# Ranking the background work of a one-core layer kernel 120 instructions behind its matmuls

## The chip, the core and the metric

The kernel runs on one core of a Trainium2 chip. The metric is the device time of one execution in microseconds (us); the time before is the median of three runs, 2014.33 us. The engines are named as in the profile: PE (TensorE, matmuls and transposes), DVE (VectorE), ACT (ScalarE), POOL (GpSimd) and SP, whose queue issues the DMAs.

## What is computed

One layer over 2048 tokens of width 1024, in float32:

```python
n = rms_norm(x, norm1_w)
q, k, v, g_lr, g_out, su, sv = split(n @ w_in)             # 256, 256, 512, 16, 512, 512, 512 columns
log_a = log_sigmoid(g_lr @ w_gate_up + b_gate_up) / 16
o = rms_norm(gla_chunked(q / 8, k, v, log_a), gla_norm_w) * silu(g_out)     # chunks of 64 tokens, state 64x128 per head
s = gelu(su) * (tril(w_s) @ layer_norm(gelu(sv)) + b_s)                     # chunks of 128 tokens
h = x + concat(o, s) @ w_out
h = h + (silu(n2 @ w_ffn_gate) * (n2 @ w_ffn_up)) @ w_ffn_down             # n2 = rms_norm(h, norm2_w)
out = rms_norm(h, final_norm_w)
```

## The kernel before

**Tiling.** The tokens are worked in four blocks of 512 rows: blocks 0 and 1, then the feed-forward part of both, then blocks 2 and 3 and theirs. A block is held transposed (`nT`, eight pieces of 128 features by 512 tokens). Each float32 operand is split into a rounded high part and a remainder: `split` (L100) casts on ACT (L104) and subtracts on DVE (L105). `mm3` (L125) makes one product from three matmuls (L128, L129, L130): low by high, high by low, high by high. Weights come by DMA into `rawp` (three buffers), their high and low parts stand in `wp` (eight buffers, four pairs). All matmul outputs share eight PSUM banks (`psp`), and a bank is free when the last engine that reads it is done.

**A block.** `mix` (L529) makes in turn the gate columns and the 16 columns of the low rank, the decay factors (`decay`, L561: two matmuls L567, then ACT and DVE in turn), k and q (`col_pair`), the products with the decay (L591, L592, L614), the values v and the output gate, a second half of the sv columns (`second_half`, L680, 128x256 outputs), then su. In blocks 1 to 3, v and the gate come from seven products instead of eight (`pair_product`, L222, in the order 1, 2, 7, 6, 4, 5, 3). The left sides of products 7, 5, 6 and 3 are sums of halves of `nT`, made step by step by `Halves.make` (L177 to L210: DVE additions L182, L196, L200, L204, L209, each followed by a split into `hop`). `drain` (L715) takes the outputs: for product 1 an ACT copy into v and for product 2 a DVE addition (L720); for product 5, once for each of two halves, an ACT copy (L731), an addition (L732) and a Silu (L733).

**The chunks.** `chunks` (L636) takes the 512 tokens in two halves. For each it makes 16 matmuls of keys by values (L645, into two banks `pu`) and 16 of scores (L654, into two banks `pq`). DVE then runs the state chain, 16 steps L663, each of which reads the step before and a piece of `pu`, and four masked copies L667 that read `pq`. `attend` (L746) multiplies states and scores (L762), normalises and transposes (L752).

**Rows to come.** `norm_rows` (L264) prepares the next block: for each 128 rows a squared sum on ACT, a scaling on DVE (L246) into one of two buffers `xsu`, eight transposes on PE (L253) and two splits of the PSUM outputs (ACT L104 and DVE L105, into `nTh` and `nTl`). The same generator serves the rows that go into the feed-forward part.

**What sets the order.** `norm_rows`, `Halves.make`, `decay`, `chunks`, `attend`, the sums of weights (L474) and others are generators in the list `bg`. `tick()` (L66) advances each of them by one step after each group of products; `finish` (L71) runs one to its end. When the program is built, a list scheduler fixes the order of every engine: of the instructions that its own estimate of times has ready, the one that stands first in program order goes first. On the chip each engine takes its instructions in that order, and each waits on semaphores for what it reads or overwrites. The start of the program (L341 to L401) is written out in the order of the work: a 4 KB row of norm weights is spread over the partitions by two matmuls (L364) and two copies (L366), with matmuls of zeros (`idling`, L357) around them.

Of the kernel before, what the change touches and what calls it, by code (L numbers as in the profile page):

```python
# [33 lines left out]
def hybrid_block(ctx, tc, x, norm1_w, w_in, w_gate_up, b_gate_up, gla_norm_w, sg_ln_w, sg_ln_b,  # L34
# [21 lines left out]
    def tpt(name, dt=F32):  # L56
        return tp.tile([P, 512], dt, name=name, tag="tp")
# [5 lines left out]

    bg = []

    def tick():  # L66
        for g in list(bg):
            if next(g, bg) is bg:
                bg.remove(g)

# [4 lines left out]

    def start(g):
        bg.append(g)
        return g

# [259 lines left out]
    n1 = sum(c for _, c in first_cols)  # L339
    blank = tpt("blank", BF16)  # L340
    nc.vector.memset(blank, 0.0)  # L341
    one_row = tpt("one")[0:1, :P]
    nc.vector.memset(one_row, 1.0)
    n1w = nwp.tile([P, D], F32, name="nw", tag="nw")
    nc.sync.dma_start(n1w[0:1, :], norm1_w[0].unsqueeze(0))
    hx = dma_x(x2, 0, [0])
    raws = []
    for t, (k0, kk) in enumerate(first_k):
# [5 lines left out]
        dma_x(x2, 0, [t + 1], hx)  # L354
    idle = ps()

    def idling(n):  # L357
        for _ in range(n):
            nc.tensor.matmul(idle, lhsT=blank[:, :P], rhs=blank, start=True, stop=True)

    idling(8)
    pw = [ps(), ps()]
    for i in range(2):
        nc.tensor.matmul(pw[i], lhsT=one_row, rhs=n1w[0:1, i * 512:(i + 1) * 512], start=True, stop=True)  # L364
    for i in range(2):
        nc.scalar.copy(n1w[:, i * 512:(i + 1) * 512], pw[i])  # L366
    idling(4)
    nT = Act(KD, "nT")
    xsu = bigt(F32, "xsu").rearrange("p (c a) b -> p c (a b)", c=2)
    first_w = []  # L370

# [10 lines left out]

    r0 = row_rstd(hx[0])
    for i in range(2):
        cs = slice(i * 512, (i + 1) * 512)
        nc.vector.scalar_tensor_tensor(xsu[:, 0, cs], hx[0][:, cs], r0, n1w[:, cs], ALU.mult, ALU.mult)
    first_split(raws[0])
    for i in range(2):
        first_put(0, i)
        idling(4)  # L390
    norm_prep(hx[1], n1w, xsu[:, 1])
    first_split(raws[1])
    first_split(raws[2])

# [7 lines left out]

    start(first_rows())

# [124 lines left out]
    def mix(blk, nT, first_w):  # L529
# [6 lines left out]
        def first_done(t, acc):  # L536
            g = glr[:, t]
            hi = sm.tile([P, RANK], F32R, name="glrhi")
            nc.scalar.copy(hi, acc[:, 256:256 + RANK])
            nc.vector.tensor_copy(g[:, 0:RANK], f32(hi))  # L540
            nc.vector.tensor_copy(g[:, 64:64 + RANK], f32(hi))
            nc.vector.tensor_tensor(g[:, 32:32 + RANK], acc[:, 256:256 + RANK], f32(hi), ALU.subtract)
            nc.scalar.activation(sv[:, t, 0:256], acc[:, 0:256], AF.Gelu)
            start(glr_put(t, g))

# [15 lines left out]
        def decay():  # L561
            yield
            if blk:
                yield
            pks = [ps(), ps()]
# [18 lines left out]

        g_dec = start(decay())

# [124 lines left out]
        else:  # L711
            gw = bigt(F32, "gw")
            started = []

            def drain(m, th, acc):  # L715
                lo, hi = th, 2 + th
                if m == 1:
                    nc.scalar.copy(v[:, lo, :], acc)
                elif m == 2:
                    nc.vector.tensor_tensor(v[:, lo, :], acc, v[:, lo, :], ALU.add)  # L720
                elif m == 7:
                    nc.scalar.copy(gw[:, hi, :], acc)
                elif m == 6:
                    nc.scalar.copy(v[:, hi, :], acc)
                elif m == 4:
                    nc.vector.tensor_tensor(v[:, hi, :], acc, v[:, hi, :], ALU.add)
                    if th:
                        started.append(chunks_start())
                elif m == 5:
                    x = tpt("x")  # L730
                    nc.scalar.copy(x, acc)  # L731
                    nc.vector.tensor_tensor(gw[:, hi, :], x, gw[:, hi, :], ALU.add)  # L732
                    nc.scalar.activation(gw[:, hi, :], gw[:, hi, :], AF.Silu)  # L733
                else:
                    gate_done(lo, acc)
# [48 lines left out]

        g_att = start(attend())

# [31 lines left out]
    def project(blk, hx, mixT, g_att, put, outer, ahead=None):  # L818
# [7 lines left out]
        def out_done(t, acc):  # L826
            residual(hx, 1, acc, t)
            r = blk * NB + t * P
            nc.sync.dma_start(hd[r:r + P, :], hx[t])
            if outer:  # L830
                gens.append(start(norm2_put(t, norm_prep(hx[t], n2w))))

# [80 lines left out]
    def gate_up(s, act):  # L913
# [59 lines left out]
        def run(late):  # L973
            for at, (key, _, m) in enumerate(seq):
                ahead(at + AHEAD + 1)
                if at == len(seq) - 5:
                    start(late)
                made[key].mul(m)
# [145 lines left out]
    for s in range(2):  # L1124
# [56 lines left out]

        start(first_operands())
        ahead, run = gate_up(s, tm)
# [13 lines left out]

        start(last_operands())
        d_start, d_run = down(s)
# [47 lines left out]
```

## Time and profile before

| | |
|---|---|
| median of three runs | 2014.33 us (2013.3 to 2014.34) |
| the profiled execution | 2013.45 us, of which the span is 2011.7 us and 1.75 us lie around it |
| PE busy | 1979.5 us, 98% of the span, mean granted clock 0.994 |
| DVE busy | 1493.7 us, 74% |
| ACT busy | 894.2 us, 44% |
| POOL busy | 86.2 us, 4% |
| DMA | 328.69 MB, mean 163 GB/s |

An engine is busy while an instruction runs on it. The start of one instruction to the start of the next on the same engine is what it costs there when nothing waits; the printed duration of a matmul is longer, since matmuls overlap. "idle before <-releaser" at a row is the time for which the engine waited in front of it, and the instruction that ended the wait. The clock is the granted share of TensorE's full 2.4 GHz; the lower of its two levels is 1.2 GHz.

### The profile page before, as it was taken

The page shows a single profiled execution, that of the slowest core. Times are in us where ns is not written, and L with a number is a line of the kernel's source. Part 1 is how long each engine was busy: PE and PEld are TensorE (multiplying, and loading weights), DVE is VectorE, ACT ScalarE, POOL GpSimd, SP SyncE. Part 2 cuts the span into 40 slices and gives each one's busy share as a digit, 9 for nine tenths or more (in the row PEclk, how much of TensorE's full clock was granted, in tenths as well). Part 3 has the DMA queues.
Part 4 walks back from the last instruction along what each step waited for, and adds up shares of the span by engine and source line. Part 5 has one row for each costly group of instructions (what it writes and reads, how often), then busy time and mean ns, then how long its engine had stood idle before and what let it go on. Part 6 is the DMA issues. An engine that isn't in the chain of part 4 may idle for free.

```text
span 2011.7 us, 26653 instructions
## 1 busy us (share of the span) xinstructions
PE 1979.5 (98%) x9861; PEld 1649.4 (82%) x9861; DVE 1493.7 (74%) x2516; ACT 894.2 (44%) x1475; POOL 86.2 (4%) x118
## 2 busy tenths in 40 slices
PE   8999899999999999999999998999999999999998
PEld 6888778888888888888887887887888888888887
DVE  6666887798987777655798758758977877776476
ACT  4544645453333333443565536446433333334343
POOL 2010101000000000000110101000000000000000
PEclk9999999999999999999999999999999999999999
DMA  6645385526663333865756444623332332367554
GB/s 211 179 159 167 137 266 175 189 89 195 219 204 97 120 98 127 302 199 179 246 181 202 137 129 155 210 84 112 114 115 94 105 115 95 100 209 266 189 190 176
DMA packets 216577, 328.69 MB, mean 163 GB/s; under 512 B 16712, under 2 KB 117630, under 8 KB 215424
## 3 DMA queue, kind: packets, MB, share of 16 engines
q1 hardware_dynamic: 216448, 327.00, 50.1%
q8 instruction: 77, 1.26, 0.3%
q14 instruction: 52, 0.43, 0.1%
HBM read 245.69 MB, written 77.07 MB: 160 GB/s over the span
## 4 chain that ended last, share of the span: by engine, by line
PE 85%; DVE 7%; ACT 4%; DMA 2%; issue 2%; POOL 0%; DVEq 0%; POOLq 0%; ACTq 0%; SPq 0%
PE ps L129 27%; PE ps L128 27%; PE ps L130 27%; DMA raw<-ad 1%; PE ps L762 1%; PE ps L253 1%; DVE b L1194 1%; DVE wlo L105 1%; DVE op L105 1%; DVE hx L1047 1%; ACT whi L104 1%; PE ps L800 1%; DMA raw<-in_w_ffn_down_dram 0%; DVE aop L105 0%; DVE sw L872 0%
## 5 line engine op out<-in xcount | busy, mean ns | idle before, releaser
L104 ACT CAST whi<-raw 128x1024 fp32r<-128x1024 f32 (+2 forms) x193 | 194.1, 1008 | 310.2 <-PE ps L129 138.2
L105 DVE TENSOR_TENSOR wlo<-raw,whi 128x1024 fp32r<-128x1024 f32 (+2 forms) x193 | 224.4, 1168 | 140.5 <-ACT whi L104 133.2
L129 PE MATMUL ps<-wlo,aop 128*128 128x512 f32 x552 | 215.1, 390 | 0.2 <-DVE wlo L105 0.2
L128 PE MATMUL ps<-whi,aop 128*128 128x512 f32 x552 | 215.1, 390 | 0.0
L130 PE MATMUL ps<-whi,aop 128*128 128x512 f32 x552 | 214.9, 389 | 0.0
L104 ACT CAST op<-sw 128x512 fp32r<-128x512 f32 x176 | 107.3, 621 | 210.6 <-DVE sw L872 190.4
L105 DVE TENSOR_TENSOR aop<-raw,aop 128x1024 fp32r<-128x1024 f32 x76 | 86.5, 1139 | 89.3 <-ACT aop L104 89.1
L105 DVE TENSOR_TENSOR op<-sw,op 128x512 fp32r<-128x512 f32 x176 | 120.2, 686 | 36.0 <-ACT op L104 35.8
L129 PE MATMUL ps<-wlo,nTh 128*128 128x512 f32 (+2 forms) x392 | 129.9, 331 | 12.0 <-DVE wlo L105 12.0
L128 PE MATMUL ps<-whi,nTl 128*128 128x512 f32 (+2 forms) x392 | 129.6, 332 | 3.2 <-DVE nTl L105 2.2
L130 PE MATMUL ps<-whi,nTh 128*128 128x512 f32 (+2 forms) x392 | 129.3, 330 | 0.0
L104 ACT CAST aop<-raw 128x1024 fp32r<-128x1024 f32 x76 | 74.5, 983 | 121.8 <-DMA raw<-ad 120.5
L129 PEld LDWEIGHTS ps<-wlo,aop 128*128 128x128 f32 x552 | 103.6, 188 | 22.0 <-DVE wlo L105 0.8
L128 PEld LDWEIGHTS ps<-whi,aop 128*128 128x128 f32 x552 | 103.7, 188 | 21.6
L130 PEld LDWEIGHTS ps<-whi,aop 128*128 128x128 f32 x552 | 103.7, 188 | 21.4
L105 DVE TENSOR_TENSOR op<-raw,op 128x512 fp32r<-128x512 f32 x132 | 88.5, 686 | 26.5 <-ACT op L104 25.9
L897 ACT COPY p<-ps 128x512 f32<-128x512 f32 x88 | 51.4, 587 | 127.4 <-PE ps L130 124.4
L128 PE MATMUL ps<-whi,mixTl 128*128 128x512 f32 x256 | 101.4, 396 | 0.9 <-DVE mixTl L105 0.9
L128 PE MATMUL ps<-nTh,wlo 128*128 128x512 f32 x256 | 101.8, 397 | 0.0
L925 ACT ACTIVATE cg<-cg 128x512 f32<-128x512 f32 x88 | 55.6, 632 | 100.1 <-DVE cg L924 100.0
L129 PE MATMUL ps<-nTl,whi 128*128 128x512 f32 x256 | 99.9, 390 | 0.0
L130 PE MATMUL ps<-nTh,whi 128*128 128x512 f32 x256 | 99.8, 390 | 0.0
(273 smaller groups left out, 5001.0 us busy)
## 6 DMA issues: line engine op xcount, KB each, us to landing
raw<-in_w_in_dram SPq DMA_DIRECT2D x66, 512.0 KB, 4.6
raw<-ad SPq DMA_DIRECT2D x64, 512.0 KB, 3.8
raw<-in_w_ffn_gate_dram SPq DMA_DIRECT2D x44, 512.0 KB, 3.9
raw<-in_w_ffn_up_dram SPq DMA_DIRECT2D x44, 512.0 KB, 3.8
raw<-td SPq DMA_DIRECT2D x35, 512.0 KB, 4.3
ad<-cg SPq DMA_DIRECT2D x66, 256.0 KB, 2.0
ad<-cs SPq DMA_DIRECT2D x22, 768.0 KB, 3.6
hx<-in_x_dram SPq DMA_DIRECT2D x32, 512.0 KB, 6.7
```

The costliest lines, as they stand in the source:

```text
L104: nc.scalar.copy(hi, src)
L105: nc.vector.tensor_tensor(lo, src, f32(hi), ALU.subtract)
L128: nc.tensor.matmul(o, lhsT=ll, rhs=rh, start=first, stop=False, skip_group_check=shared)
L129: nc.tensor.matmul(o, lhsT=lh, rhs=rl, start=False, stop=False, skip_group_check=shared)
L130: nc.tensor.matmul(o, lhsT=lh, rhs=rh, start=False, stop=last, skip_group_check=shared)
L253: nc.tensor.transpose(pt[:, k * P:(k + 1) * P], xs[:, (4 * i + k) * P:(4 * i + k + 1) * P], ident)
L762: nc.tensor.matmul(pos[hh][c * CH:(c + 1) * CH, (2 * i + p) * DV:(2 * i + p + 1) * DV], lhsT=left[:, hh, p, n * CH:(n + 1) * CH], rhs=righ ...
L800: nc.tensor.matmul(pm[:, t * P:(t + 1) * P], lhsT=sv[:, t, g * P:(g + 1) * P], rhs=wsT[:, g, :], start=True, stop=True)
L897: nc.scalar.copy(t[m], o)
L925: nc.scalar.activation(g, g, AF.Silu)
L1047: nc.vector.tensor_tensor(h[i, l], h[i, l], y, ALU.add)
L1194: nc.vector.tensor_tensor(*(b[:, k] for b in args[:3]), args[3])
```

## The change

Each step that `tick()` makes is put 120 places further back in the order by which the scheduler chooses, save for generators that are started as urgent. These are the first rows, the transposes of the low rank (`glr_put`), `decay`, `attend`, the second norm of blocks 1 and 3 (`norm2_put`) and the late operands of the feed-forward part. `decay` drops one step in blocks 1 to 3. In `drain` of product 5 both ACT copies come ahead of both additions. The start is written inside `tc.manual_schedule()`, which keeps the written order on each engine: the norm weights come as one DMA to all partitions (512 KB), the matmuls L364 and copies L366 go, and 24 matmuls of zeros stand where 20 stood.

```diff
+    LATER = 120
+    bg, urgent = [], []
     def tick():
         for g in list(bg):
-            if next(g, bg) is bg:
-                bg.remove(g)
+            with tc.high_priority(offset=0 if g in urgent else -LATER):
+                if next(g, bg) is bg:
+                    bg.remove(g)
...
-    def start(g):
+    def start(g, now=False):
         bg.append(g)
+        if now:
+            urgent.append(g)
...
-    n1w = nwp.tile([P, D], F32, name="nw", tag="nw")
-    nc.sync.dma_start(n1w[0:1, :], norm1_w[0].unsqueeze(0))
-    hx = dma_x(x2, 0, [0])
...
-    idling(8)
-    pw = [ps(), ps()]
-    for i in range(2):
-        nc.tensor.matmul(pw[i], lhsT=one_row, rhs=n1w[0:1, i * 512:(i + 1) * 512], start=True, stop=True)
-    for i in range(2):
-        nc.scalar.copy(n1w[:, i * 512:(i + 1) * 512], pw[i])
-    idling(4)
...
+    with tc.manual_schedule():
+        blank = tpt("blank", BF16)
+        nc.vector.memset(blank, 0.0)
+        hx = dma_x(x2, 0, [0])
+        n1w = norm_w(norm1_w[0])
+        first_load(*first_k[0])
+        first_load(*first_k[1])
+        dma_x(x2, 0, [1], hx)
+        first_load(*first_k[2])
+        dma_x(x2, 0, [2, 3], hx)
...
+        idling(18)
+        r0 = row_rstd(hx[0])
...
+        first_put(0, 0)
+        idling(3)
+        nc.vector.tensor_tensor(lo, raws[0], f32(hi), ALU.subtract)
+        first_w.append((hi, lo))
+        first_put(0, 1)
+        idling(3)
+        first_split(raws[1])
+        norm_prep(hx[1], n1w, xsu[:, 1])
+        first_split(raws[2])
...
-    start(first_rows())
+    start(first_rows(), True)
...
-            start(glr_put(t, g))
+            start(glr_put(t, g), True)
...
         def decay():
             yield
-            if blk:
-                yield
...
-        g_dec = start(decay())
+        g_dec = start(decay(), True)
...
                 elif m == 5:
-                    x = tpt("x")
-                    nc.scalar.copy(x, acc)
-                    nc.vector.tensor_tensor(gw[:, hi, :], x, gw[:, hi, :], ALU.add)
-                    nc.scalar.activation(gw[:, hi, :], gw[:, hi, :], AF.Silu)
+                    kept.append(tpt("x"))
+                    nc.scalar.copy(kept[th], acc)
+                    for i in range(2) if th else ():
+                        g = gw[:, 2 + i, :]
+                        nc.vector.tensor_tensor(g, kept[i], g, ALU.add)
+                        nc.scalar.activation(g, g, AF.Silu)
...
-        g_att = start(attend())
+        g_att = start(attend(), True)
```

Lines of the changed kernel are numbered five higher up to `decay`, three higher from there to the `drain` of product 5, and five higher behind it: L110 is the subtraction L105, L187, L205, L209 and L214 are the additions L182, L200, L204 and L209, L258 is the transpose L253, L648 and L657 are the chunk products L645 and L654, L666 is the step of the state chain L663, L723 is the addition L720.

At three places the orders stand as follows. The first is DVE in block 1, between the left operands of the chunks and the additions of product 2 to the values. `hs` and `nw` are scratch of `Halves`, `hop` a made left side, `wlo` the low part of a weight. Before:

```order
L204 TENSOR_TENSOR nw<-nw,hs 128x1024
L591 TENSOR_TENSOR eu<-ps,eu 128x512
L592 TENSOR_TENSOR eu_2097<-ps,eu_2097 128x512
L105 TENSOR_TENSOR hop<-nw,hop 128x1024
L614 SCALAR_TENSOR_TENSOR left<-ps,eu 64x512 x4
L105 TENSOR_TENSOR wlo<-raw,whi 128x1024
L209 TENSOR_TENSOR hs<-hs,nw 128x1024
L105 TENSOR_TENSOR wlo<-raw,whi 128x1024 x2
L105 TENSOR_TENSOR hop<-hs,hop 128x1024
L105 TENSOR_TENSOR wlo<-raw,whi 128x1024
L720 TENSOR_TENSOR v<-ps,v 128x512 x2
```

Now, the twelve rows that follow `left`, `wlo`, `hop` and two more `wlo`:

```order
L187 TENSOR_TENSOR nw<-nTh_1538,nTl_1540 128x1024
L110 TENSOR_TENSOR wlo<-raw,whi 128x1024
L205 TENSOR_TENSOR nw<-nw,hs 128x1024
L110 TENSOR_TENSOR wlo<-raw,whi 128x1024
L187 TENSOR_TENSOR hs<-nTh_1538,nTl_1540 128x1024
L110 TENSOR_TENSOR hop<-nw,hop 128x1024
L110 TENSOR_TENSOR wlo<-raw,whi 128x1024
L209 TENSOR_TENSOR nw<-nw,hs 128x1024
L214 TENSOR_TENSOR hs<-hs,nw 128x1024
L110 TENSOR_TENSOR wlo<-raw,whi 128x1024
L723 TENSOR_TENSOR v<-ps,v 128x512 x2
L110 TENSOR_TENSOR hop<-nw,hop 128x1024
```

The steps of `Halves` that stood ahead of the left operands stand behind them, and so do four more `wlo`; the two additions L723 and the `hop` of product 6 come last.

The second is PE in block 1 around the chunk products (x16 is 16 in a row). Before, for the first half; the second half stood 48 matmuls of products 5 and 3 (three to a row of `mm3`, all left operand `hop`) further back, and then the 128x256 outputs of `second_half`:

```order
L130 MATMUL ps<-whi,nTh_1539 128x512
L623 MATMUL ps<-ident,eu_2097 128x128 x2
L645 MATMUL ps<-v,eu_2097 64x128 x16
L654 MATMUL ps<-left,eu 64x64 x16
L128 MATMUL ps<-whi,hop 128x512
L129 MATMUL ps<-wlo,hop 128x512
```

Now:

```order
L134 MATMUL ps<-wlo,hop 128x512
L135 MATMUL ps<-whi,hop 128x512
L648 MATMUL ps<-v,eu_2096 64x128 x13
L657 MATMUL ps<-left,eu 64x64 x16
L648 MATMUL ps<-v,eu_2096 64x128 x16
L657 MATMUL ps<-left,eu 64x64 x16
L133 MATMUL ps<-whi,nTl_1539 128x256
L134 MATMUL ps<-wlo,nTh_1537 128x256
```

Both halves stand behind product 3, next to each other, ahead of `second_half`; three of the L648 of the first half stand ahead of product 6.

The third is PE at the transition from block 0 to block 1. Before, the last of four groups of eight transposes, the other three of which stood 24 matmuls apart in front of it:

```order
L128 MATMUL ps<-whi,mixTl_1245 128x512
L129 MATMUL ps<-wlo,mixTh_1243 128x512
L130 MATMUL ps<-whi,mixTh_1243 128x512
L253 MATMUL ps<-ident,xsu 128x128 x8
L128 MATMUL ps<-whi,nTl_1540 128x272
L129 MATMUL ps<-wlo,nTh_1538 128x272
```

Now:

```order
L133 MATMUL ps<-whi,mixTl_1244 128x512
L134 MATMUL ps<-wlo,mixTh_1242 128x512
L135 MATMUL ps<-whi,mixTh_1242 128x512
L258 MATMUL ps<-ident,xsu 128x128 x29
L133 MATMUL ps<-whi,nTl_1539 128x272
L134 MATMUL ps<-wlo,nTh_1537 128x272
```

The transposes of all four groups of rows but three stand in one piece between the output projection of block 0 and the first columns of block 1. The transition from block 2 to block 3 reads the same.

## Rows read from the trace of the kernel before

**Rows 1.** The page, busy time of each engine and its share of the span

```profile
PE 1979.5 (98%) x9861; PEld 1649.4 (82%) x9861; DVE 1493.7 (74%) x2516; ACT 894.2 (44%) x1475; POOL 86.2 (4%) x118
```

**Rows 2.** The page, chain that ended last, by engine

```profile
PE 85%; DVE 7%; ACT 4%; DMA 2%; issue 2%; POOL 0%; DVEq 0%; POOLq 0%; ACTq 0%; SPq 0%
```

**Rows 3.** Timeline of PE, blocks 1 to 3: start us, us, instruction, [idle before <-releaser]

```profile
227.56 0.71 PE L567 MATMUL ps<-glrT,wup 96*128 96x512 f32 x2
...
251.57 0.80 PE L129 MATMUL ps<-wlo,nTh 128*128 128x512 f32 x1 [4.77 <-DVE wlo L105]
252.16 0.63 PE L130 MATMUL ps<-whi,nTh 128*128 128x512 f32 x1
252.59 0.63 PE L128 MATMUL ps<-whi,nTl 128*128 128x512 f32 x1
...
288.59 0.50 PE L128 MATMUL ps<-whi,hop 128*128 128x512 f32 x1 [2.56 <-ACT x L731]
...
1067.57 0.76 PE L129 MATMUL ps<-wlo,nTh 128*128 128x512 f32 x1 [2.48 <-DVE wlo L105]
1243.68 0.80 PE L129 MATMUL ps<-wlo,nTh 128*128 128x512 f32 x1 [4.77 <-DVE wlo L105]
1403.52 0.47 PE L129 MATMUL ps<-t3l,op 128*128 128x512 f32 x1 [1.56 <-ACT op L104]
```

**Rows 4.** Stretches: length; busy us (xcount) of PE, PEld, DVE, ACT, POOL; PE clock; DMA

```profile
240.00:260.00 20.00, 14.86 (x59) 11.71 (x57) 17.86 (x23) 12.18 (x16) 0.00 (x0) 0.83 0.57 214
1060.00:1080.00 20.00, 17.01 (x68) 13.22 (x67) 17.24 (x27) 12.84 (x19) 1.73 (x1) 0.91 0.46 154
1400.00:1420.00 20.00, 18.44 (x82) 14.99 (x81) 20.00 (x34) 8.29 (x15) 0.00 (x0) 1.00 0.16 54
```

**Rows 5.** Timeline of PE, transition from block 0 to block 1

```profile
200.47 0.39 PE L130 MATMUL ps<-whi,mixTh 128*128 128x512 f32 x1
200.70 1.03 PE L253 MATMUL ps<-ident,xsu 128*128 128x128 f32 x8
201.49 0.37 PE L128 MATMUL ps<-whi,nTl 128*128 128x272 f32 x1
```

**Rows 6.** Timeline of DVE, same transition

```profile
203.31 1.28 DVE L105 TENSOR_TENSOR nTl<-ps,nTh 128x512 fp32r<-128x512 f32 x2
204.51 1.28 DVE L246 SCALAR_TENSOR_TENSOR xsu<-hx,st,nw 128x1024 f32<-128x1024 f32 x1
```

**Rows 7.** Timeline of DVE, block 1: left operands and the value additions

```profile
246.32 1.23 DVE L105 TENSOR_TENSOR hop<-nw,hop 128x1024 fp32r<-128x1024 f32 x1
247.47 2.79 DVE L614 SCALAR_TENSOR_TENSOR left<-ps,eu 64x512 f32<-64x512 f32 x4
...
257.66 0.69 DVE L720 TENSOR_TENSOR v<-ps,v 128x512 f32<-128x512 f32 x1
```

**Rows 8.** Timeline of DVE, block 1: state chain and masks of one half

```profile
279.96 2.99 DVE L663 SCALAR_TENSOR_TENSOR right<-right,dec,ps 64x128 f32<-64x128 f32 x8
282.87 0.92 DVE L667 COPY_PREDICATED left<-keep,ps 64x256 f32<-64x256 int32 x2
```

**Rows 9.** Timeline of PE, block 1: both sorts of chunk product, then the next columns

```profile
293.12 1.16 PE L645 MATMUL ps<-v,eu 64*64 64x128 f32 x32
294.05 1.15 PE L654 MATMUL ps<-left,eu 64*64 64x64 f32 x32
295.13 0.39 PE L128 MATMUL ps<-whi,nTl 128*128 128x256 f32 x1
```

**Rows 10.** Timeline of PE, block 0: one transpose between large products

```profile
45.80 0.48 PE L128 MATMUL ps<-nTh,wlo 128*128 128x512 f32 x1
46.12 0.40 PE L129 MATMUL ps<-nTl,whi 128*128 128x512 f32 x1
```

**Rows 11.** Timeline of PE, start of the program

```profile
4.80 3.78 PE L364 MATMUL ps<-nw,one 1*128 1x512 f32 x4
...
13.27 1.04 PE L380 MATMUL ps<-ident,xsu 128*128 128x128 f32 x8
```

More of the change, by code (lines that the diff above doesn't have):

```diff
@@ L60, in f32 @@
         return ap.bitcast(F32)
-    bg = []
+    LATER = 120
+    bg, urgent = [], []
     def tick():
         for g in list(bg):
-            if next(g, bg) is bg:
-                bg.remove(g)
+            with tc.high_priority(offset=0 if g in urgent else -LATER):
+                if next(g, bg) is bg:
+                    bg.remove(g)
     def finish(g):
@@ L339, in hybrid_block, with first_load @@
     n1 = sum(c for _, c in first_cols)
[L340 to L343, printed above, removed]
-    n1w = nwp.tile([P, D], F32, name="nw", tag="nw")
-    nc.sync.dma_start(n1w[0:1, :], norm1_w[0].unsqueeze(0))
-    hx = dma_x(x2, 0, [0])
-    raws = []
-    for t, (k0, kk) in enumerate(first_k):
+    nT = Act(KD, "nT")
+    xsu = bigt(F32, "xsu").rearrange("p (c a) b -> p c (a b)", c=2)
+    raws, first_w = [], []
+    def first_load(k0, kk):
         raw, o = view(rawp, F32, "raw", kk, n1), 0
@@ L353, in hybrid_block @@
         raws.append(raw)
[L354 to L359, printed above, removed]
-    idling(8)
-    pw = [ps(), ps()]
-    for i in range(2):
-        nc.tensor.matmul(pw[i], lhsT=one_row, rhs=n1w[0:1, i * 512:(i + 1) * 512], start=True, stop=True)
-    for i in range(2):
-        nc.scalar.copy(n1w[:, i * 512:(i + 1) * 512], pw[i])
-    idling(4)
-    nT = Act(KD, "nT")
-    xsu = bigt(F32, "xsu").rearrange("p (c a) b -> p c (a b)", c=2)
-    first_w = []
     def first_split(raw):
@@ L381, in first_put, with idling @@
         nT.put(i, t, pt)
[L383 to L393, printed above, removed]
+    with tc.manual_schedule():
[8 more added lines that the diff above has]
+        dma_x(x2, 0, [2, 3], hx)
+        idle = ps()
+        def idling(n):
+            for _ in range(n):
+                nc.tensor.matmul(idle, lhsT=blank[:, :P], rhs=blank, start=True, stop=True)
+        idling(18)
+        r0 = row_rstd(hx[0])
+        for i in range(2):
+            cs = slice(i * 512, (i + 1) * 512)
+            nc.vector.scalar_tensor_tensor(xsu[:, 0, cs], hx[0][:, cs], r0, n1w[:, cs], ALU.mult, ALU.mult)
+        hi, lo = (view(wp, F32R, n, first_k[0][1], n1) for n in ("whi", "wlo"))
+        nc.scalar.copy(hi, raws[0])
+        first_put(0, 0)
[7 more added lines that the diff above has]
+        first_split(raws[2])
     def first_rows():
@@ L712, in mix @@
             gw = bigt(F32, "gw")
-            started = []
+            started, kept = [], []
             def drain(m, th, acc):
@@ L830, in out_done @@
             if outer:
-                gens.append(start(norm2_put(t, norm_prep(hx[t], n2w))))
+                gens.append(start(norm2_put(t, norm_prep(hx[t], n2w)), True))
         def hook(t, k0):
@@ L976, in run @@
                 if at == len(seq) - 5:
-                    start(late)
+                    start(late, True)
                 made[key].mul(m)
@@ L1180, in first_operands @@
             operand(2, b1[1])
-        start(first_operands())
+        start(first_operands(), True)
         ahead, run = gate_up(s, tm)
@@ L1196, in last_operands @@
                 yield
-        start(last_operands())
+        start(last_operands(), True)
         d_start, d_run = down(s)
```

## The prediction

> **What bounds the kernel now.** I read the busy times first, then the chain that ended last, then PE's waits and the stretches around them. PE is busy for 98% of the span [rows 1] and makes 85% of the chain [rows 2], so whatever stops PE adds to the time, and work elsewhere costs something only where PE waits for it. PE's longer waits behind the start are few, and four of them stand where this change moves instructions [rows 3]: 4.77 us in block 1 and again in block 3, and 2.48 in block 2, each for the low part of the weight of product 2, and 2.56 in block 1 for the copy of a shared sum. A wait costs more than itself. The stretch with the first wait of 4.77 us has a granted clock of 0.83, the one with 2.48 us has 0.91, that is 0.09 of 20 us lost, or 1.8, and one with a wait of 1.56 us keeps 1.00 [rows 3, 4]. In the first, matmuls of 512 columns start 0.43 us apart after the wait [rows 3] instead of 0.23 [rows 5], which is the lower level of the clock. I price a fall of the clock at 2 us, and let one follow a wait of over 2 us.
>
> **The transitions between blocks.** Before, the transposes of the next block's rows stand in eights between the projections of the old block, and PE goes on after the last eight without idle [rows 5]. Now 29 stand in one piece. Their inputs share two buffers, so the scaling of rows 2 (counting from 0) waits for the transposes of rows 0, and rows 3 for rows 1. What was spread beside 72 products becomes one chain through DVE. From the end of the projection, by the new DVE order: a weight's low part ends at about 1.9 us, since its cast on ACT ends at 0.8 and it takes 1.15; two low parts of `nT` at 0.6 each (two in 1.2, [rows 6]) end at 3.0; the scaling at 1.2 [rows 6] ends at 4.2. PE has made its 16 transposes by 1.75, at 0.1 each [rows 5], and idles for 2.5. Eight more end at 5.1; the next scaling has two more low parts ahead of it and ends at 6.6, so PE idles again for 1.5. That is 4.0 us and one fall of the clock, 6 each for the transitions from block 0 to 1 and from 2 to 3: **+12**. The transition from block 1 to 2 has the same knot among the last products of the feed-forward part, where some are left to fill it; by the same rows two waits of 1.0 and 0.75: **+1.75**. The bounds are 0, if DVE's earlier work is done before the projection ends, and 8 per transition.
>
> **Block 1, up to product 6.** I count from the two matmuls of `decay` (227.56, [rows 3]). Before, the left operands L614 ended at 250.3 [rows 7], 22.7 us later, and ahead of them since `decay` stood two `hop` and one addition, 1.15 each [rows 7]. Those three now stand behind, so the left operands end at about 19.3, the weight of product 2 at 20.6, and PE, which reaches it after 84 matmuls at 0.23 and a few transposes at 20.4, waits 0.3 instead of 4.77. But from there DVE has 13 instructions of 1.15 in a row, 15 us, ahead of the first value addition, which ends at 36.3 (0.69 printed, about 0.6 from start to start); the second ends at 36.9 and the `hop` of product 6 at 38.1. PE has by 30.2 made the rest of product 2 (2.5), product 7 (24 matmuls, 5.4), and the transposes of the keys, with some short waits. Then the three chunk products that now stand there wait for the addition, 6.1 us, and product 6 another 1.2. Without those three, product 6 would still hold PE to 38.1, so the wait does not hang on them. The bounds: 2 us, if the left operands end five sooner, and 9.
>
> **Block 1, the chunks.** PE makes 13 + 16 + 16 + 16 chunk products, at 0.93 us for 16 of the one sort and 1.08 of the other [rows 9], in 3.85. `second_half` then needs banks that the state chain frees. DVE can begin at 0.5, and has 12 steps at 0.36 (eight in 2.91, [rows 8]), two weights at 1.15 and a wait of about 0.7 for the cast of one of them: 7.9. PE idles for 4.0 and its clock falls. Before, 48 large products lay between the two halves (11 us) and the first chain went on beside them. The bounds are 1 and 6 us. The copies ahead of the additions do away with the wait of 2.56. Block 1 thus idles 0.3 + 6.1 + 1.2 + 4.0 = 11.6 in place of 7.3, with two falls as before: **+4.3**.
>
> **Blocks 3 and 2.** Block 3 has the order of block 1, and idled only 4.8 at this place, with one fall: 6.8 more and a second fall, **+8.8**. In block 2 the steps of `Halves` are further along. The wait of 2.48 goes; the `hop` of product 6 comes 2.4 late, and the bank wait is 13 steps and one weight (5.9, from 0.5 on) against 4.0 of PE, another 2.4. Idle 4.8 for 2.5, and a second fall: **+4.3**.
>
> **The rest.** The start loses the matmuls L364 (3.7 us to the next start); the first transposes stand at 13.27 [rows 11]. The squared sum can now begin when the first rows of x land, but 512 KB of norm weights come ahead of the first weights, which delays the products behind. I take **-3**, bounds -4 and +2. About 130 more places have a small matmul alone between large ones. A transpose alone cost 0.03 + 0.32 - 0.23 = 0.12 [rows 10] against 0.10 in a group of eight [rows 5], so I take **0** for them; 13 us if each lost 0.1. Casts, subtractions and DMAs are the same in number, beside PE, and hidden by it.
>
> The sum is 12 + 1.75 + 4.3 + 8.8 + 4.3 - 3 = 28.15 on the profiled execution's 2013.45, so 2041.6; the median stands 0.9 higher. I forecast **2042 us**, with 2028 to 2050 as this case's own range.
>
> **The rivals.** (1) *The waits go and none comes.* If DVE is far enough ahead when the left operands end, as `decay` is urgent and a step sooner, the value additions and the `hop` are in time and the chains overlap. What decides is whether the 15 us of DVE fit beside the 10 us that PE has there. Then the four waits (14.6) and their falls (8) go, and with the start 2014 - 25.6 + 13.75 for the transitions gives about 2002. For it speaks that DVE has 26% idle [rows 1]; against it, that the instructions were only moved to where it has none. Chance 0.13. (2) *The chunks wait less,* as the weights between the steps come early or late: 16 less, 2026; 0.13. (3) *Short waits cost clock too.* The row with 1.56 us of wait keeps a clock of 1.00 [rows 4], and by it the small waits cost only themselves. Five such waits with a fall each would add 10: 2052; 0.08. The Trainium skill (TensorE: Matmul & The Clock Gate, A second HAM failure mode: psum-queue depth-cycling) says that a kernel which cycles through PSUM banks can idle so often between groups of matmuls that its clock swings between the two levels; this program would become such a case, and the row of 1.56 us speaks against it. (4) *Small matmuls between large ones cost 0.1 each:* 2055; 0.06. (5) *Gains and losses meet* near 2014, as the late steps fall into slack that PE leaves elsewhere; 0.05. That the change does not do what it says is excluded by the orders. My forecast has 0.55.
>
> **The numbers.** A difference of 0.2%, 4 us, is about what a measurement of this kernel can tell from none. Rival 1 and 0.02 of rival 5 give faster, 0.15; 0.03 of rival 5 and 0.02 of the lower end of rival 2 give the same, 0.05; the rest is slower, 0.80. A range from 2010 to 2054 leaves out rival 1 and the end of 4.
>
> **What would show it.** In the changed profile: PE idle in front of a transpose at the transitions, near 205 and 1195 us, released by the scaling; in blocks 1 and 3 a wait of about 6 us for the value addition L723 and none over 1 us for the low part of product 2; a wait of 2 to 4 us of the first 128x256 product for L666, with a granted clock under 0.95; no wait for the copy of x; the first transposes near 10 us. If PE meets none of these waits and its busy time is as before, the forecast is wrong, and rival 1 right. If the time is over 2050 with no longer waits, the pitch of large matmuls beside single small ones tells rivals 3 and 4 apart.

## The result and the profile after

The changed kernel takes 2110.77 us (median of four runs, 2106.36 to 2111.37) beside 2013.82 us (2013.04 to 2014.34) for the kernel before on the same chip: a ratio of 1.0477, interval 1.0459 to 1.0495. It is slower by 97 us, where 2042 was forecast. The direction was right; the size was not, and the time lies far above the range.

The page of the changed kernel, busy time of each engine, against [rows 1]:

```profile
PE 2039.6 (97%) x9861; PEld 1665.2 (79%) x9861; DVE 1497.3 (71%) x2515; ACT 896.9 (43%) x1473; POOL 87.1 (4%) x118
```

The profiled execution took 2111.19 us, its span is 2109.5 us (before 2011.7) and its mean clock 0.983 (before 0.994). PE has as many instructions as before and is busy for 60.1 us longer (2039.6 - 1979.5). It idles for 69.9 us (2109.5 - 2039.6) where it idled for 32.2, 37.7 more. So only two fifths of the 97.8 us between the two spans are waits: **PE needs longer for the same matmuls.** Where it waits, the view of waits of the changed kernel tells (total us, times, longest):

```profile
PE ps L133 <- DVE right L666: 12.5, 3, 4.4
PE ps L648 <- DVE v L723: 11.9, 2, 6.0
PE ps L258 <- DVE xsu L251: 7.9, 4, 2.8
PE ps L134 <- DVE wlo L110: 3.8, 4, 1.1
PE ps L469 <- POOL wraw L461: 3.4, 1, 3.4
PE ps L133 <- DVE mixTl L110: 3.0, 5, 1.0
...
PE ps L258 <- DVE nTl L110: 2.7, 1, 2.7
```

The first three are the state chain, the value additions and the scaling of the forecast. The timeline of PE in the changed kernel shows one of each, and two stretches that no term of the forecast covered (start, us, instruction, [idle before]):

```profile
7.60 0.60 PE L364 MATMUL ps<-ident,xsu 128*128 128x128 f32 x4
...
118.52 0.50 PE L134 MATMUL ps<-wlo,nTh 128*128 128x512 f32 x1
118.95 0.33 PE L657 MATMUL ps<-left,eu 64*64 64x64 f32 x2
119.21 0.49 PE L135 MATMUL ps<-whi,nTh 128*128 128x512 f32 x1
...
137.06 0.49 PE L134 MATMUL ps<-nTl,whi 128*128 128x512 f32 x1
137.49 0.43 PE L767 MATMUL ps<-right,left 128*64 128x128 f32 x2
137.85 0.49 PE L135 MATMUL ps<-nTh,whi 128*128 128x512 f32 x1
...
224.03 1.40 PE L258 MATMUL ps<-ident,xsu 128*128 128x128 f32 x8 [2.81 <-DVE xsu L251]
...
277.92 0.50 PE L134 MATMUL ps<-wlo,nTh 128*128 128x512 f32 x1 [1.12 <-DVE wlo L110]
...
294.00 1.11 PE L648 MATMUL ps<-v,eu 64*64 64x128 f32 x6 [5.88 <-DVE v L723]
...
328.10 0.58 PE L133 MATMUL ps<-whi,nTl 128*128 128x256 f32 x1 [4.25 <-DVE right L666]
```

What such a matmul costs in a row of its own kind, the timeline of PE in the kernel before shows for the products of the state:

```profile
128.71 1.97 PE L762 MATMUL ps<-right,left 128*64 128x128 f32 x32
130.60 0.50 PE L128 MATMUL ps<-nTh,wlo 128*128 128x512 f32 x1
```

The profile records one such float32 matmul twice, so x2 is one and x32 are 16, and each costs 0.12 (1.89 / 16).

Here the new cost can be read, by the pitch, the time from one start to the next. Near 118 and 137 us single scores (L657) and single products of the state (L767) stand between large matmuls, with no idle. A product of the state starts at 137.49 and the next large one at 137.85, 0.36 later; the large one, which takes 0.23 in a run [rows 5], is followed only 0.43 later (137.06 to 137.49). Together that is 0.36 + 0.43 - 0.23 = 0.56 for a matmul that costs 0.12 in its row: **0.44 us lost.** A score takes 0.26 (118.95 to 119.21) and 0.43 (118.52 to 118.95) less 0.23, against 0.07 in a row of 16 (1.08 / 16, [rows 9]): **0.39 lost.** Counted over the whole timeline, the products of the state stand in 83 pieces, some 20 in each block, where there were two to a block; the scores of block 0 stand in 24 pieces where there were 2.

The weight loads (PEld) go with that time. The timeline of PEld in the changed kernel:

```profile
137.49 0.19 PEld L767 LDWEIGHTS ps<-right,left 128*64 128x64 f32 x2 [0.24 <-issue]
137.85 0.19 PEld L135 LDWEIGHTS ps<-nTh,whi 128*128 128x128 f32 x1 [0.17 <-issue]
```

Each load starts at the time of its own matmul. In a run of large matmuls a load starts with the matmul ahead of it (an example stands with e8). At each change of kind the load is thus exposed, going in and coming out.

Such a stretch looks healthy otherwise. Stretches of the changed kernel (length; busy us of PE, PEld, DVE, ACT, POOL; PE clock; DMA), and then the first one in the kernel before:

```profile
100.00:120.00 20.00, 20.00 (x94) 15.13 (x92) 14.55 (x33) 4.70 (x5) 1.08 (x2) 1.00 0.51 157
220.00:240.00 20.00, 16.19 (x111) 15.56 (x109) 12.53 (x24) 7.86 (x16) 1.06 (x2) 0.83 0.37 129
```

```profile
100.00:120.00 20.00, 20.00 (x144) 16.55 (x143) 17.20 (x57) 4.94 (x6) 4.12 (x4) 1.00 0.20 58
```

In the first stretch PE is 100% busy at a clock of 1.00 in both kernels. Neither number shows the loss; the pitch does. Of the large matmuls the changed kernel begins 74 there and the kernel before 78, and that one makes 32 chunk products besides, where the changed one makes nine scores. The second row holds the waits near 224 us, and there the clock falls as in [rows 4], to 0.83.

What the clock costs can be added up. Over all stretches with the lower level, PE is busy for 53.0 us in the changed kernel and for 18.8 before; large matmuls start 0.43 us apart there instead of 0.23 [rows 3, 5], so about half of that is lost, 26.5 and 9.4, and **17.1 us of PE's longer busy time are the clock**; 43.0 are left. Behind the start there are ten falls where there were four.

### The profile page after: what moved, and what is told of

Same layout as the page of the kernel before. It is cut to its first block, busy times and chain, and to the rows that moved or that the text cites. A ratio compares the mean times of both kernels' runs of the same rounds, so it can differ in the third digit from the quotient of the medians.

```text
span 2109.5 us, 26645 instructions
## 1 busy us (share of the span) xinstructions
PE 2039.6 (97%) x9861; PEld 1665.2 (79%) x9861; DVE 1497.3 (71%) x2515; ACT 896.9 (43%) x1473; POOL 87.1 (4%) x118
## 4 chain that ended last, share of the span: by engine, by line
PE 84%; DVE 7%; DMA 4%; ACT 3%; issue 1%; POOL 0%; SPq 0%; DVEq 0%; POOLq 0%; ACTq 0%
PE ps L134 27%; PE ps L133 27%; PE ps L135 27%; PE ps L767 2%; DMA raw<-in_w_in_dram 1%; DMA raw<-ad 1%; DVE wlo L110 1%; ACT whi L109 1%; PE ps L258 1%; DVE right L666 0%; DMA raw<-vd 0%; DMA raw<-in_w_ffn_up_dram 0%; DVE nTl L110 0%; DVE xsu L251 0%; DVE left L617 0%
## 5 line engine op out<-in xcount | busy, mean ns | idle before, releaser
L110 DVE TENSOR_TENSOR wlo<-raw,whi 128x1024 fp32r<-128x1024 f32 (+2 forms) x192 | 223.7, 1169 | 168.8 <-ACT whi L109 156.7
L110 DVE TENSOR_TENSOR aop<-raw,aop 128x1024 fp32r<-128x1024 f32 x76 | 86.5, 1139 | 93.8 <-ACT aop L109 93.6
L133 PE MATMUL ps<-whi,nTl 128*128 128x512 f32 (+2 forms) x392 | 135.2, 345 | 15.2 <-DVE right L666 12.5
L110 DVE TENSOR_TENSOR op<-sw,op 128x512 fp32r<-128x512 f32 x176 | 120.1, 685 | 37.1 <-ACT op L109 36.7
L110 DVE TENSOR_TENSOR op<-raw,op 128x512 fp32r<-128x512 f32 x132 | 88.5, 685 | 27.5 <-ACT op L109 27.1
L134 PE MATMUL ps<-nTl,whi 128*128 128x512 f32 x256 | 105.3, 411 | 0.0
L135 PE MATMUL ps<-nTh,whi 128*128 128x512 f32 x256 | 105.2, 411 | 0.0
L134 PE MATMUL ps<-wlo,mixTh 128*128 128x512 f32 x256 | 100.8, 394 | 0.0
```

Source lines behind the costliest of these rows:

```text
L110: nc.vector.tensor_tensor(lo, src, f32(hi), ALU.subtract)
L133: nc.tensor.matmul(o, lhsT=ll, rhs=rh, start=first, stop=False, skip_group_check=shared)
L134: nc.tensor.matmul(o, lhsT=lh, rhs=rl, start=False, stop=False, skip_group_check=shared)
L135: nc.tensor.matmul(o, lhsT=lh, rhs=rh, start=False, stop=last, skip_group_check=shared)
```

## The experiments

Each run numbers the lines of its own kernel, a few apart from those above; the names of the tiles tell which line is meant.

**First: which part.** The theory was that small matmuls alone between large ones cost the missing time, and that they come from the urgent steps: a step in a context with offset 0 gets ranks that the products written behind it get again, since the rank count is set back at the end of the context; the two then alternate. The rival was that the steps ranked 120 behind do all of it, through waits.

*e1_urgent_plain*: the change, with the urgent steps outside any context.

```diff
-            with tc.high_priority(offset=0 if g in urgent else -LATER):
+            if g in urgent:
+                if next(g, bg) is bg:
+                    bg.remove(g)
+                continue
+            with tc.high_priority(offset=-LATER):
```

> The changed kernel with one edit: urgent background steps are emitted without a priority context, so that the products written after them rank behind them and not beside them. By the order the 128 state products L767 then stand in 8 runs of 16 instead of 83 runs, and the singles of scores fall from 30 runs to 26. Theory S (a small matmul alone between large ones costs about 0.44 us for a state product and 0.39 for a score, as its neighbours start 0.2 us late on either side): 75 x 0.44 + 4 x 0.39 = 34 us less, 2077 us, with PE's busy time down by as much and the long waits as in the changed kernel. Theory W (the 97 us are waits and the clock falls behind them, singles cost 0.1 at most): 8 us less or fewer, over 2100 us.

Measured: 2061.59 us beside 2015.52 (ratio 1.0231, 1.0209 to 1.0253), 49 less than the change. PE is busy for 1997.8 us, 41.8 less, and the products of the state stand in rows of 16 again. The urgent steps' context costs half of the 97 us; the rest remains, the single scores of block 0 among it, with the waits for the state chain and the scaling as in the changed kernel, and the one for the value additions down from 11.9 to 3.7. The waits of e1:

```profile
PE ps L137 <- DVE right L670: 13.3, 3, 4.7
PE ps L262 <- DVE xsu L255: 7.8, 4, 2.8
...
PE ps L630 <- DVE v L727: 3.7, 2, 2.1
```

*e2_no_rank*: the change, with `tick()` as before, so that the start, the earlier decay and the copies of the sums stay.

```diff
-            with tc.high_priority(offset=0 if g in urgent else -LATER):
-                if next(g, bg) is bg:
-                    bg.remove(g)
+            if next(g, bg) is bg:
+                bg.remove(g)
```

> The changed kernel without any ranking: all background steps are emitted in place, as before the change. The new start, the decay one step sooner and the early copies of the shared sums remain. Theory: the ranking alone makes the loss, so the time is at or below that of the kernel before: the start gives 2.4 us up to the first decay matmuls (48.97 against 51.35 us), the wait of 2.56 us for the copy in block 1 and its clock fall go (4.5 us), the decay one step sooner gives between 0 and 4: 2004 to 2010 us. Rival (the start, the decay or the copies carry a part of the loss): over 2016 us.

Measured: 2013.35 us (0.999, 0.998 to 1.0). I had expected a few us of gain and could not resolve one. The three other parts together are worth nothing that can be measured; the wait for the low part of product 2 stays at 12.6 us in four.

*e3_attend_tied*: the kernel before, with only the steps of `attend` in a context of offset 0.

```diff
     def tick():
         for g in list(bg):
+            if g in tied:
+                with tc.high_priority(offset=0):
+                    if next(g, bg) is bg:
+                        bg.remove(g)
+                continue
...
         g_att = start(attend())
+        tied.append(g_att)
```

> The kernel before with one edit: the steps of attend alone are emitted in a priority context of offset 0, so that they tie in rank with the products behind them. By the order the state products L762 stand in 80 runs instead of 8 and transposes in 105 runs instead of 65; nothing else is ranked back. Theory S: 72 x 0.44 = 32 us more, 2045 us, almost all of it as busy time of PE; the transposes alone cost nothing. Theory W (only waits and clock falls cost): within 5 us of the kernel before.

Measured: 2048.32 us (1.0158, 1.0134 to 1.0182). The page of e3:

```profile
PE 2013.4 (98%) x9861; PEld 1648.7 (80%) x9861; DVE 1494.0 (73%) x2516; ACT 896.2 (44%) x1475; POOL 86.5 (4%) x118
```

No instruction is added and none is ranked behind. The clock is 0.994 as before and the idle time 35.6 us (32.2 before), yet PE is busy for 33.9 us longer. The products of the state are broken into 72 more runs, and the transposes of `attend` into 40 more. At 0.03 a transpose (by e8, below) these make 1.2 us, and (33.9 - 1.2) / 72 = 0.45 is left for each of the 72, beside the 0.44 from the pitch. A part of its timeline of PE:

```profile
132.09 0.49 PE L134 MATMUL ps<-nTl,whi 128*128 128x512 f32 x1
132.51 0.43 PE L767 MATMUL ps<-right,left 128*64 128x128 f32 x2
132.87 0.50 PE L135 MATMUL ps<-nTh,whi 128*128 128x512 f32 x1
133.21 0.40 PE L133 MATMUL ps<-nTh,wlo 128*128 128x512 f32 x1
```

The first large matmul behind a small one takes 0.42 us if another small one follows, 0.34 if a large one does. So one term of the sum, worth 34 us by itself, is shown without the clock and with only 3.4 us of idle time beside it.

*e4_rank_only*: the kernel before with the ranking alone (`LATER`, the context in `tick()`, the urgent generators), and none of the other parts.

> The kernel before with the ranking alone: steps 120 behind, urgent ones with offset 0; the old start, the old step count of decay and the old order of copies and additions. Theory: this carries the whole loss and lacks the small gains of the rest, so 2110 to 2120 us, with the same waits for the value addition, the hop, the state chain and the scaling at the transitions. Rival (the sooner decay or the early copies make the waits in blocks 1 and 3): under 2095 us.

Measured: 2109.76 us (1.0471, 1.0451 to 1.0491), the change's own time within a microsecond. With e2 this splits the change cleanly: the ranking is all of its loss.

**Second: what the other half is, and what a small matmul costs.** *e5_norm_plain* is e1 with the three `norm_rows` generators in place; *e6_chunks_plain* is e1 with the steps of `chunks` and of the keys' transposes in place.

```diff
...
-        g_n1 = start(norm_rows(hx1, nT.put, norm_w(norm1_w[0]), 3))
+        g_n1 = start(norm_rows(hx1, nT.put, norm_w(norm1_w[0]), 3), True)
...
```

```diff
...
-            return start(chunks())
+            return start(chunks(), True)
...
```

> The kernel of the run e1 with the generators of the next rows (norm_rows) also emitted in place, so that their transposes stand in eights between the projections again. Theory T (the 29 transposes in one piece hold PE at the transitions): the waits for the scaling (7.8 us in four) and for the low part of the rows at the transition to block 2 (3.1) go, and three falls of the clock at 2 us: 2061.6 - 17 = 2045 us. Rival (these waits are made up elsewhere, since DVE is then late for the left operands): 2055 us or more.

> The kernel of the run e1 with the chunk products and the transposes of the keys (chunks, kend_put) also emitted in place, so that the two halves of a block's chunk products stand apart again and the scores stand in 10 runs and not 26. Theory: the waits for the state chain (13.3 us in three) and for the copy of the state (2.4) go, with three falls of the clock (6), and 16 runs of scores less at 0.39 (6): 2061.6 - 28 = 2034 us, with PE waiting for the hop of product 6 where it waited for the value addition. Rival (the banks are late whichever way, as DVE is behind in these blocks): 2050 us or more.

Measured: 2031.1 us (1.0085, 1.0061 to 1.0109) and 2029.93 us (1.0076, 1.0055 to 1.0096). Each takes 30.5 and 31.7 us from e1; both gain more than I expected. In e5 PE idles for 15.9 us less than in e1 and is busy for 13.9 less, with the clock up from 0.988 to 0.993. In e6 it idles for 18.0 us less and is busy for 12.9 less; there the scores of block 0 stand in rows again.

*e8_alone*: the kernel before, with small matmuls added at 224 places, 28 for each of eight kinds. Each goes alone (the eighth kind in pairs) into the middle of 12 large ones of the feed-forward part, to a bank that nobody reads. It adds work and takes none away.

```diff
             for k in range(4):
                 mm3(o, (wh[:, k], wl[:, k]), (th[:, k], tl[:, k]), k == 0, k == 3)
+                if extra and k == 1:
+                    extra()
...
```

> The kernel before with 224 extra small matmuls, each alone between two large ones of the gate and up products, whose outputs nobody reads; eight kinds of 28: plain float32 128x128, plain float32 with a 128x64 left side (the shape of a state product), plain float32 64x64 (a score), a transpose of 128x128, the float32r form with a 96x128, a 96x64 and a 64x64 left side, and two 128x64 plain ones in a row. Theory S1 (the price is that of a left side narrower than the array, of 64 columns or 64 rows): the 128x128 kind and the transpose cost about 0.1 us, every kind with 64 in it 0.35 to 0.45, whatever its type. Theory S2 (the price is that of the plain float32 form, which runs in two passes, between float32r products): every plain kind costs 0.3 to 0.45, every float32r kind and the transpose 0.1 or less. The pair costs 0.12 more than the single by both.

Measured: a span of 2097.4 us, 85.7 more, in a single execution. Medians, in us, worked out from the timeline: from the large matmul ahead to the small one, from there to the next large one, and all the time that the small one adds, over the three large pitches behind it too:

```
kind (weights rows*columns)    large -> small   small -> large   added
float32, 128*128                    0.23             0.14          0.23
float32, 128*64                     0.32             0.36          0.57
float32, 64*64                      0.32             0.26          0.46
transpose, 128*128                  0.24             0.03          0.13
float32r, 96*128                    0.23             0.06          0.13
float32r, 96*64                     0.23             0.06          0.13
float32r, 64*64                     0.32             0.20          0.40
two of float32, 128*64              0.32             0.58          0.80
```

Times 28 the last column adds up to 80 us; PE is busy for 82.4 us longer than before (2061.9 - 1979.5). Every kind has the same price at all its 28 places, within 0.01 us.

Here is the row that misled me: the transpose adds 0.13, as in [rows 10], and it is one of the three cheapest kinds. The kinds that the change set alone, 128*64 and 64*64 in float32, are the two dearest single ones. Both simple theories fall: 64 columns alone cost nothing more (float32r, 96*64, adds what 96*128 does), and float32 alone (128*128) adds 0.23, not 0.3 to 0.45. A second 128*64 behind the first adds 0.23 more, where I expected the 0.12 of a row; why is open. The timeline of PE in e8 at one 128*64, one transpose and one float32r of 64*64:

```profile
512.35 0.39 PE L130 MATMUL ps<-t2h,op 128*128 128x512 f32 x1
512.67 0.43 PE L925 MATMUL ps<-ident 128*64 128x128 f32 x2
513.03 0.50 PE L128 MATMUL ps<-t2h,op 128*128 128x512 f32 x1
...
694.28 0.40 PE L130 MATMUL ps<-t2h,op 128*128 128x512 f32 x1
694.52 0.27 PE L929 MATMUL ps<-ident 128*128 128x128 f32 x1
694.54 0.48 PE L128 MATMUL ps<-t2h,op 128*128 128x512 f32 x1
...
1617.75 0.27 PE L935 MATMUL ps<-wup 64*64 64x128 f32 x1
```

And the loads of the same matmuls, from the timeline of PEld:

```profile
512.13 0.19 PEld L130 LDWEIGHTS ps<-t2h,op 128*128 128x128 f32 x1
512.67 0.19 PEld L925 LDWEIGHTS ps<-ident 128*64 128x64 f32 x2 [0.35 <-DVE cs L968]
513.03 0.19 PEld L128 LDWEIGHTS ps<-t2h,op 128*128 128x128 f32 x1 [0.17 <-issue]
...
694.28 0.14 PEld L929 LDWEIGHTS ps<-ident 128*128 128x128 f32 x1
694.52 0.19 PEld L128 LDWEIGHTS ps<-t2h,op 128*128 128x128 f32 x1
...
1537.17 0.13 PEld L933 LDWEIGHTS ps<-wup 96*64 96x64 f32 x1
...
1617.75 0.13 PEld L935 LDWEIGHTS ps<-wup 64*64 64x64 f32 x1 [0.35 <-issue]
```

The load of the transpose starts at 694.28, with the large matmul ahead of it, 0.24 before its own: it is hidden. So is that of the float32r matmul of 96*64, at 1537.17 (its matmul starts at 1537.40). The load of the 128*64 and of the 64*64 starts with its own matmul (512.67, 1617.75). The load of the large L130 at 512.13 starts 0.22 ahead of its matmul, the load of L128 at 513.03 with it. All 28 matmuls of a kind do the same. The loads of float32 of 128*128, of the transpose and of both 96-row kinds start 0.22 to 0.24 us ahead of their matmuls; those of 128*64, single or in pairs, and of 64*64, in float32 or float32r, start with them. What is hidden and what is not thus goes with the kind: the four kinds with a hidden load add 0.13 to 0.23, the others 0.40 and more. That the load is the cause is my reading of this, and by which property the chip decides, these eight kinds do not settle.

*e9_halves_early*: e2, with the two empty steps at the head of `Halves.make` taken away, to start its chain earlier instead of later.

```diff
             a, b, c = spare
-            yield
-            yield
             whole(a, 0, 0)
```

> The kernel of the run e2 (no ranking) with the steps of Halves begun two ticks sooner, so that DVE makes four of its sums and two of its splits where it idled before the decay. If what PE waits for in blocks 1 and 3 (4.8 us each for the low part of product 2) is DVE's load between the decay and the left operands, about 3.4 us of it go in each of the two blocks and with them most of the clock falls: 2013.4 - 9 = 2004 us. Rival (the sums now delay the transposed low rank and so the decay itself): 2010 us or more.

Measured: 2008.06 us (0.9963, 0.9951 to 0.9975), 4 above what I expected and below both kernels. The wait for the low part falls, but is not gone:

```profile
PE ps L133 <- DVE wlo L109: 8.7, 3, 3.6
```

**Third: a version without the loss.** *e10_norm_chunks_plain* is e1 with the edits of e5 and of e6, so that of the long chains only `Halves` and the sums of weights are ranked behind.

> The kernel of the run e1 with both edits of e5 and e6: next rows, chunks and keys emitted in place, so that of the ranked steps none with matmuls of its own is left but the constants; the steps of Halves, the weight sums and the second norm of sv stay 120 behind, and the state, score and transposing products stand in the runs of the kernel before. If the two losses are independent, 2061.6 - 30.5 - 31.7 = 1999 us, and what stays ranked gains, since DVE does the weights first. Rival (the loads of DVE are the same and only change places, so the rest of the ranking is worth nothing): 2009 to 2015 us, like e2.

Measured: 2006.89 us (0.9962, 0.9948 to 0.9975; twelve runs), 54.7 below e1 where 30.5 and 31.7 add to 62.2; with intervals of 3 to 5 us on each of the four times, the 7.5 between them may be noise. The page and the first waits of e10:

```profile
PE 1974.8 (98%) x9861; PEld 1647.0 (82%) x9861; DVE 1493.5 (74%) x2515; ACT 893.1 (45%) x1473; POOL 90.5 (5%) x118
```

```profile
PE ps L137 <- DVE hop L114: 4.1, 2, 2.1
...
PE ps L138 <- DVE wlo L114: 3.4, 4, 1.2
```

The wait for the low part is down to 3.4 us from 12.2 in the kernel before, at the price of two waits of 2 us for a `hop`. PE's busy time is back at 1974.8.

*e11_both_early* is e10 with the edit of e9; *e12_only_sums* is e10 with `Halves` in place too; *e13_sums_early* is e12 with the edit of e9.

```diff
-            self.made = start(self.make())
+            self.made = start(self.make(), True)
```

> The kernel of the run e10 with the steps of Halves begun two ticks sooner, as in e9. If a step ranked 120 behind is still taken when DVE idles, they move ahead of the decay as in e9 and the time falls by 5 to 8 us below that of e10. Rival (120 places put them behind the decay whichever tick begins them): within 3 us of e10.

> The kernel of the run e10 with the steps of Halves emitted in place too, so that only the weight sums, the second norm of sv, the constants and the loads of the residual rows are ranked behind. If their rank is worth nothing, the time is that of e2, 2013 us, within 3; if they stood in the way of the weights on DVE, 2003 to 2008. If e10 is faster than this one, the late steps of Halves are a gain, otherwise a loss.

> The kernel of the run e12 with the steps of Halves begun two ticks sooner. Against e12 this should give what e9 gave against e2, 5 us less; if the rank of the sums is a gain of its own it comes on top of e9's 2008. Rival (both free the same time of DVE): equal to e9 within 3 us.

Measured: 2007.78 (0.996, 0.9942 to 0.9977), 2016.44 (1.0008, 0.9994 to 1.0021) and 2009.3 (0.9975, 0.9962 to 0.9989). With `Halves` in place the gain of e10 is gone, so it comes from the late steps of `Halves`, which issue no matmul. For e10 I had expected 1999 if the two losses were independent, for e11 5 to 8 us less than e10; neither came. Starting `Halves` two steps earlier gives about the same (e9, e13), and both together no more (e11). Of all versions e10 has the lowest median; its interval overlaps those of e9, e11 and e13.

## Why the prediction was wrong

**The failed step** stands in the paragraph on the rest: "About 130 more places have a small matmul alone between large ones ... so I take 0 for them; 13 us if each lost 0.1." The places were found and the mechanism was listed as a rival, but the price came from a transpose and was carried over to matmuls of another kind. It stands in the timeline of PE before, just ahead of [rows 10]:

```profile
45.77 0.27 PE L549 MATMUL ps<-ident,glr 128*96 128x128 f32 x1
```

By the pitches, 75 more runs of the products of the state at 0.44 make 33 us, 22 more of scores at 0.39 make 8.6, and some 43 more of transposes at 0.03 (0.13 less the 0.10 of [rows 5]) make 1.3: about 43 us instead of 0, as many as PE's longer busy time has left without the clock. e3 shows 34 us of them directly, e8 the price by kind. A nearer row stood in the trace of before, on PE in block 0, and was not used:

```profile
104.39 0.39 PE L130 MATMUL ps<-whi,nTh 128*128 128x512 f32 x1
104.71 1.15 PE L645 MATMUL ps<-v,eu 64*64 64x128 f32 x32
105.64 1.15 PE L654 MATMUL ps<-left,eu 64*64 64x64 f32 x32
106.72 0.51 PE L128 MATMUL ps<-whi,nTl 128*128 128x512 f32 x1
107.06 0.40 PE L129 MATMUL ps<-wlo,nTh 128*128 128x512 f32 x1
```

The large matmul ahead of the chunk products takes 0.32 us and the one behind them 0.34, instead of 0.23: a switch to this kind and back costs at least 0.09 + 0.11 = 0.20, twice the bound that I took, and what the last small one loses is hidden in its row.

**The waits came as forecast.** Scaling at the transitions 0 to 1 and 2 to 3: 7.9 us, forecast 8.0. Value additions: 11.9, forecast 12.2. State chain: 12.5, forecast 10.4. Block 1 alone: 1.12 + 5.88 + 4.25 = 11.25, forecast 11.6, though the `hop` of product 6 cost nothing and the low part 0.8 more. In block 2, PE waits 2.43 us at a product with `hop`, forecast 2.4; the profile names the ACT copy L679, which ended at 1125.63, but the `hop` itself ended at 1125.51 (1124.29 and 1.22 on DVE), so either would have held PE that long. Transition 1 to 2: 2.7, forecast 1.75. The start: the first transposes at 7.60 instead of 13.27, and the decay of block 0 at 48.97 instead of 51.35, a gain of 2.4 against 3.

**The rest of the gap.** Idle time grew by 37.7 us against 23.15 in the forecast. Among the 14.5 between them are the state chain (2.1 over its forecast), the wait for POOL's L461 in block 0 (3.4, before 1.1) and the low parts of `mixT` (3.0, before 0.9); the rest are shorter waits, most of about 1 us, which were not set against the forecast one by one. PE's busy time grew by 60.1; less 43 for the small matmuls, 17 are left for the clock, where I took 8, and the busy time at the lower level gives the same 17.1 by itself. I had four falls more and six came, and one cost 2.5 us and not 2: the two that I had not forecast stand at the transition 1 to 2 and, near 1484 us, behind three waits of 0.5 to 1.0. So 43 + 14.5 + 9 + 3 (the start's gain, which I had subtracted as a term of its own and the measured totals already hold) is the gap of 69.6 between 97.8 and 28.15, to the rounding.

**What the experiments give back.** Undoing the transitions and the chunks alone gave 30.5 and 31.7 us, where my terms for them sum to 13.75 and 17.4. The idle time alone fell by 15.9 and 18.0; the clock, and in e6 the scores, make the rest. How it splits between them was not worked out.

**The rivals.** Rival 4 was the right mechanism at under a third of its size (13 us of 43), and its place was right: the sign that I gave for telling it from rival 3, the pitch of large matmuls beside single small ones, is what settled it. Rival 3 had little to do with it: the stretches with alternating matmuls keep a clock of 1.00, and e3 keeps 0.994 over 72 such places; one of the ten falls behind the start, the one near 1484 us, does follow short waits only. Rivals 1, 2 and 5 fall with the waits, which all came.

The Trainium skill (TensorE: Matmul & The Clock Gate, Step-by-step: what each phase is for) says that PE takes a weight load ahead of running matmuls if their row groups do not conflict or the load goes to the background buffer. The loads of large matmuls and transposes, 0.22 to 0.24 us ahead, agree with it; that the other loads fail these conditions is not shown here. The rows alone do not tell the kinds apart: a float32r load of 96 rows, between large matmuls that use all 128, is hidden (0.13 added), and one of 64 rows is not (0.40).

Not tried: what keeps the loads of the 64-row kinds and of float32 128*64 from being taken ahead, where that of float32 128*128 is; the decay step and the copies of the sums each alone.

## What to carry to other kernels

Before an instruction order is loosened, list the matmuls that stand in rows of their own kind, and price a break of each row by that kind and shape (0.03 us for a transpose, 0.44 for a product of the state here), never by a transpose alone. A PE that is 100% busy at full clock can still be losing time: compare the pitch of like matmuls. Here only the steps of `Halves`, which issue no matmul, gained by standing behind (0.4%). And look at the order that a context of offset 0 gives: in e3 it alone made the scheduler alternate the steps with the products behind them. That a shared rank is the reason is my reading, not shown.

## What the chip showed that was not expected

In e8 a single small matmul between large ones costs 0.13 us as a transpose or in float32r with 96 rows, 0.23 in float32 with 128*128, 0.40 to 0.46 with 64 rows, and 0.57 in float32 with 128*64; a pair of the last costs 0.80. The large matmul behind pays part of it: 0.28 to 0.34 us instead of 0.23 in e8, and 0.42 in e3 where another small one follows it.
